# One order for VectorE's evacuations, weight sums and low parts, and an early last product in the second gate pair

## The chip, the cores and the metric

The kernel runs on one core of one Trainium2 chip. The metric is the time of one execution in microseconds (us) on the device; the kernel before takes 2360.54 us, the median of three executions. TensorE is PE in the profile, its weight loads PEld, VectorE is DVE, ScalarE is ACT, GpSimd is POOL, and SP is the engine that only issues transfers here.

## What is computed

The reference is a trunk of two layers over 512 frames of width 1024, all in fp32. What bears on the change is that nearly all of its work is matrix products of activations with weights:

```python
for i in range(DEPTH):
    h = rmsnorm(x, norm1_g[i])
    z = h @ w_in[i] + b_in[i]
    _, _, mv, mo, mi, mf, rq, rk, rv, rg, gm, gr = split_cols(z)
    ...
    hr = retention_chunkwise(rope(rq), rope(rk) / 16, rv, log_gamma)
    y_r = silu(rg) * head_layernorm(hr, r_norm_g[i], 4)
    merged = sigmoid(gm) * (y_m @ w_bm[i]) + sigmoid(gr) * (y_r @ w_br[i])
    x = x + merged @ w_out[i]
    h2 = rmsnorm(x, norm2_g[i])
    x = x + square(relu(h2 @ w_ff1[i] + b_ff1[i])) @ w_ff2[i] + b_ff2[i]
    h3 = rmsnorm(x, norm3_g[i])
    x = x + sigmoid(h3 @ w_pe_gate[i]) * (p[i] @ w_pe[i])
return rmsnorm(x, final_g)
```

Retention has four heads with values of width 512. Head h multiplies its normalised output by `silu(rg)`, 512 columns of `z`. These are the gates that the change speaks of.

## The kernel before

**Numbers in two parts.** Each fp32 operand is split into a high part in the rounded type that TensorE takes (ACT copies it, L277) and a low part, the rest (DVE subtracts, L278). A product is three matmuls: high by high, high by low, low by high. So each piece of weights, once loaded by SP into a raw tile (`wr`, four of them and at times a fifth), needs an ACT copy to `wh` and after it a DVE subtraction to `wl`. This is `prep_next` (L365), and `ready(k)` prepares pieces in one fixed list up to number k. The copies keep the order of the list among themselves, and so do the subtractions (`in_order`, L280). A raw tile is free for the next load when its last reader is through, and there are three tiles each for the high and the low parts of whole pieces, so a pair's B waits until the pair before is done with its own B.

**Units and pairs.** The weights are a list of units. T8 units (128 output columns) and V units are plain: one piece, products over all 512 frames. PAIR units cover 256 output columns and 1024 inputs as a 2 by 2 block scheme with seven half-size products in place of eight. A pair's weights are the pieces A, B, C and D (`PRODUCTS` and `PIECE`, from L91): A holds B11 and t1, B holds B21 and t2, C holds B22 and t3, D holds t4. The sums t1 and t3 are made by GpSimd transfers between DRAM tensors. For the feed-forward weights so are t2 and t4; for all other pairs (44 of the program) DVE makes t2 into B's raw tile out of the raw tiles of A and C (L379) and t4 out of B's raw tile (L381), before the ACT copy of that piece. So a pair's piece B has the chain: sum L379, copy L277, subtraction L278.

**The seven products and their banks.** `run_pair` (L433) issues P1, P5, P6, P2, P3, P7 and, later, P4. Each is twelve matmuls of 256 columns. Three PSUM banks are used: P1, P6, P7 and P4 accumulate one on top of the other in bank a, P5 and P3 in bank c, P2 is alone in bank b. After each product its bank is read out (an evacuation): in `pair_tiles` P1, P5, P6 and P4 by ACT (L476, L478, L482, L488), P2, P3 and P7 by DVE (L480, L484, L486, adding to what was read out before). The next product of a bank can't start before the evacuation of the one before is done. So P6 waits for P1's, P7 for P6's, P4 for P7's, P3 for P5's. Pieces are asked for by `READY`: ahead of P6 the next unit's first piece, ahead of P7 one piece more, which is B where the next unit is a pair.

P4 is not issued at once. It is put on the list `later`, and `flush` issues it at the next good place: in a next pair after its P1 and P5, in a T8 unit in the middle, in V units after the first, in the attention after the first rows. P4's evacuation hands the result to `consume`.

**The gates.** `r_out` (L988) makes a head's gates by two pairs, named o0 and o1 (w = 0, 1), each giving two tiles of 128 columns; `consume` puts Silu over them (ACT, L995). Then for v = 0 to 3 it transposes the head's output on TensorE (four transposes to a bank, `back`), multiplies it by gate tile v on DVE (L1006) and splits it. The last product of o1 comes with the `flush` after the transposes of v = 0. There are eight such places, four heads in two layers (l0r0o1 to l1r3o1 in the trace).

**Queries and keys.** `r_qk` makes a head's rotated queries and keys by two pairs one right behind the other, named brq and brk. `consume` is the rotation: six DVE instructions (L961 to L963) and two splits for each. Behind head 0's brk comes the gate pair bgm2.

**The feed-forward pairs.** `ff2` (L1265) is a pair whose evacuations all are DVE additions into `x` (L1272, L1274). It is named o with two numbers; l0o33 and l1o33 are the last of their layers, followed by the gate product `pg`.

**Who sets the order.** The framework in which the kernel is written lines up each engine's instructions when the program is built, by its own estimate of when each could start, and keeps the order of the code only where an edge says so. `tc.add_manual_dep(..., ORDER)` writes such an edge; it costs no wait, as both ends are on one engine. Before the change there are edges between copies, between subtractions and between weight loads. DVE's evacuations and sums have none: they can be put ahead of or behind any subtraction. [...]

Of the kernel before, what the change touches and what calls it, by code (L numbers as in the profile page):

```python
# [38 lines left out]
OP = mybir.AluOpType  # L39
SYNC = mybir.DependencyInfo(mybir.DependencyClass.Sync, mybir.DependencyReason.DATA)  # L40
ORDER = mybir.DependencyInfo(mybir.DependencyClass.NoSync, mybir.DependencyReason.DATA)
# [57 lines left out]
GIVEN = ("B11", "B12", "B21", "B22")  # L99
MADE = {"t1": ("B12", "B11"), "t3": ("B12", "B22"), "t2": ("t1", "B22"), "t4": ("t2", "B21")}  # L100

READY = {"P1": 2, "P4": 2, "P5": 3, "P2": 4, "P6": 4, "P3": 4, "P7": 5}


def due(k):
# [4 lines left out]
def in_dram(g):  # L110

    return g[1][0] == "f"
# [115 lines left out]
def build(ctx, tc, ins, out):  # L228
    nc = tc.nc
    ve, ac, gp, te = nc.vector, nc.scalar, nc.gpsimd, nc.tensor  # L230
# [17 lines left out]
    cur = {}  # L248
# [21 lines left out]
    def ps(name):  # L270
        return psum.tile([P, T], F32, name=name, tag="ps")
# [4 lines left out]
    def split(src, hi_ap, lo_ap):  # L276
        a = ac.activation(hi_ap, src, AF.Copy)  # L277
        return a, ve.tensor_sub(lo_ap, src, hi_ap.bitcast(F32))  # L278

    def in_order(kind, *new):  # L280

        for a, b in zip(cur.get(kind, ()), new):
            tc.add_manual_dep(b.ins, a.ins.name, ORDER, reason="order of the weights")
        cur[kind] = new


    index, given, sums, k = {}, {}, {}, 0
    for g, v in groups().items():
        index[g] = len(index)
# [46 lines left out]
    order = [(n, x) for n, u in enumerate(units) for x in (PIECE if u[0] == "PAIR" else (0,))]  # L336
    place = {x: k for k, x in enumerate(order)}
    loads = [(n, x) for n, u in enumerate(units) for x in (LOADS[in_dram(u[1])] if u[0] == "PAIR" else (0,))]
    raws, pieces = {}, {}
# [25 lines left out]
    def prep_next():  # L365
        n, x = order[at["prep"]]
        at["prep"] += 1
        fill_raws()

        w = Q if x == "D" else UN  # L370
        pl = cur["last"] if n >= NU - LAST else wpool
        kw = {"tag": "d", "bufs": 2} if x == "D" else {"tag": "l", "bufs": 2 * LAST} if pl is not wpool else {
            "tag": "w", "bufs": 2 * PIECES}
        out_ = [pl.tile([P, w], F32R, name=f"w{a}{n}_{x}", **kw) for a in "hl"]
        f, l = slice(0, Q), slice(Q, 2 * Q)
        if x in ("B", "C", "D") and not in_dram(units[n][1]):
            b = raws[n, "B"]
            if x == "B":
                ve.tensor_tensor(b[:, l], raws.pop((n, "A"))[:, l], raws[n, "C"][:, f], OP.add)  # L379
            elif x == "D":  # L380
                ve.tensor_tensor(b[:, f], b[:, f], b[:, l], OP.add)  # L381
            r = raws.pop((n, x)) if x == "C" else b
            if x == "D":
                del raws[n, "B"]
        elif x == "A" and not in_dram(units[n][1]):
            r = raws[n, x]
        else:
            r = raws.pop((n, x))
        in_order("prep", *split(r[:, :w], *out_))
        pieces[n, x] = out_  # L390

    def ready(k):
        while at["prep"] < min(len(order), k + 1):
            prep_next()
# [31 lines left out]
    later = []  # L426

    def flush():

        while later:  # L430
            later.pop()()

    def run_pair(name, act, done):  # L433

        n = next_unit()
        assert units[n][0] == "PAIR", units[n]
        bank = {}

        def product(x):
            w, half, j = PRODUCTS[x]  # L440
            ready(place[n, "A"] + READY[x])
            wh, wl = [a[:, half * Q:(half + 1) * Q] for a in pieces[n, w]]
            b = {"P2": "b", "P5": "c", "P3": "c"}.get(x, "a")
            first = x in ("P1", "P2", "P5")
            if first:
                bank[b] = ps(f"{name}{b}")
            o = bank[b][:, 0:S]
            for k in range(4):
                s = slice(k * P, (k + 1) * P)
                h, l = act[k](j)  # L450
                f, e = first and k == 0, k == 3
                te.matmul(o, wh[:, s], h, start=f, stop=False, skip_group_check=True)
                te.matmul(o, wh[:, s], l, start=False, stop=False, skip_group_check=True)
                cur["mm"] = te.matmul(o, wl[:, s], h, start=False, stop=e, skip_group_check=True)
            done(x, o)

        def last():
            product("P4")
            for w in PIECE:
                del pieces[n, w]  # L460

        product("P1")
        product("P5")
        flush()
        for x in ("P6", "P2", "P3", "P7"):
            product(x)
        later.append(last)

    def pair_tiles(name, act, consume, y=None):

        y = y or [tmp(f"{name}y{d}") for d in range(2)]
        a, b = slice(0, S), slice(S, T)

        def done(x, o):
            if x == "P1":
                ac.activation(y[0][:, b], o, AF.Copy)  # L476
            elif x == "P5":
                ac.activation(y[1][:, a], o, AF.Copy)  # L478
            elif x == "P2":
                ve.tensor_tensor(y[0][:, b], o, y[0][:, b], OP.add)  # L480
            elif x == "P6":
                ac.activation(y[1][:, b], o, AF.Copy)  # L482
            elif x == "P3":
                ve.tensor_tensor(y[1][:, b], o, y[1][:, b], OP.add)  # L484
            elif x == "P7":
                ve.tensor_tensor(y[1][:, a], o, y[1][:, a], OP.add)  # L486
            else:
                ac.activation(y[0][:, a], o, AF.Copy)  # L488
                consume(y)

        run_pair(name, act, done)

    def pair_operand(name, st, hi, lo):

# [120 lines left out]
    def bcol(i, n, k):  # L615
        o, _ = _B[n]
        return bc[:, i, o + k:o + k + 1]
# [185 lines left out]
    x = big("x0", F32)  # L803
# [17 lines left out]
    for i in range(L):  # L821
# [166 lines left out]
        def r_out(h, num, y):  # L988
            nm = f"l{i}r{h}o"
            gs = {}  # L990

            def gates(w):
                def consume(g):
                    for d in range(2):
                        ac.activation(g[d], g[d], AF.Silu, bias=bcol(i, "brg", 4 * h + 2 * w + d), scale=SIGN[d])  # L995
                        gs[2 * w + d] = g[d]

                return consume

            for w in range(2):  # L1000
                pair_tiles(f"{nm}{w}", xs, gates(w))
            for v in range(4):
                o = back(nm, num, v)
                if v == 0:
                    flush()
                ve.scalar_tensor_tensor(gs[v], o, bcol(i, "grn", 4 * h + v), gs[v], OP.mult, OP.mult)  # L1006
                split(gs[v], y[0][(4 * h) % 8 + v], y[1][(4 * h) % 8 + v])

# [41 lines left out]
        for d in range(4):  # L1050
            o = t8(xa, f"l{i}m0z{d}")
# [7 lines left out]
            a = (f"l{i}m0{d}", 8 * (d // 2) + d % 2, qk[2 * (d // 2)][d % 2], qk[2 * (d // 2) + 1][d % 2], d < 2, n1)  # L1059
# [24 lines left out]
        xs = sevenfold(xn, xs_t)  # L1084
# [55 lines left out]
        for c in range(KT):  # L1140
            o = t8(yr, f"l{i}br0{c}")
# [20 lines left out]
        for c in range(KT):  # L1162
# [6 lines left out]
            o = t8(yr, f"l{i}br1{c}")  # L1169
# [13 lines left out]
        if i == L - 1:  # L1183
            x_pool = phase("x", act_side)
            whole = x_pool.tile([P, KT, T], F32, name=f"l{i}x", tag="x")
            x = [whole[:, c, :] for c in range(KT)]
        else:
            x = big(f"l{i}x", F32)
# [17 lines left out]
        for c in range(KT):  # L1206
            o = t8((mh, ml), f"l{i}wo{c}")
# [54 lines left out]
        def tile3(c):  # L1262
            n3.tile(c, x[c])

        def ff2(b, p):  # L1265
            started = set()

            def add(q, o, op):
                y = x[2 * p + q // 2][:, (q % 2) * S:(q % 2 + 1) * S]
                if b == 0 and q not in started:  # L1270
                    started.add(q)
                    ve.scalar_tensor_tensor(y, y, bcol(i, "bf2", 2 * p + q // 2), o, OP.add, op)  # L1272
                else:
                    ve.tensor_tensor(y, y, o, op)  # L1274

            def done(x_, o):
                if x_ in ("P1", "P2"):
                    add(1, o, OP.add)
                elif x_ == "P5":
                    add(2, o, OP.subtract)  # L1280
                elif x_ in ("P6", "P3"):
                    add(3, o, OP.subtract)
                elif x_ == "P7":
                    add(2, o, OP.subtract)
                elif x_ == "P4":
                    add(0, o, OP.add)
                    if b == 3 and p == 3:
                        tile3(6)
                        tile3(7)
                if b == 3 and p and x_ in ("P6", "P7"):  # L1290
                    tile3(2 * p - 2 + (x_ == "P7"))

            def parts(k):
                h, l = hid[b, k]
                return lambda j: (h[:, j * S:(j + 1) * S], l[:, j * S:(j + 1) * S])

            run_pair(f"l{i}o{b}{p}", [parts(k) for k in range(4)], done)
# [20 lines left out]
        for u in range(2):  # L1318
            _, wh, wl = unit("PE")
            for c in range(4):  # L1320
                o = ps(f"l{i}pe{u}{c}")
# [11 lines left out]
        last = i == L - 1  # L1333
# [21 lines left out]
        for c in range(KT - LAST if last else KT):  # L1355
            o = t8(n3.act, f"l{i}pg{c}")
# [27 lines left out]
    for a, n in enumerate(nn):  # L1384
        for c in range(KT - LAST, KT):
            _, wh, wl = ws[c - KT + LAST]
            o = ps(f"pl{a}{c}")[:, :256]
# [134 lines left out]
```

## Time and profile before

| | |
|---|---|
| executions | 2364.43, 2360.54, 2360.48 us |
| span of the profiled execution | 2365.7 us (the page gives no other time of it) |
| TensorE busy | 2333.0 us, 99% |
| VectorE busy | 1697.9 us, 72% |
| ScalarE busy | 1256.4 us, 53% |
| granted TensorE clock, mean | 0.996 |

The profile is of one more execution, beside the three that were timed. Busy time is the union of an engine's instructions; a wait shows as idle time. "<-" names what ended an idle time. In names of tiles buffer numbers are left out, so `wr<-wr,wr` is a weight sum of whichever pair, and `wh_B`, `wl_B` are the high and low part of a piece B.

### The profile page before, as it was taken

To read this page: it belongs to the slowest core of one execution; us is meant where nothing else is said; L and a number is where in the kernel's file an instruction comes from. 1 tells how busy PE (TensorE), PEld (TensorE's weight loads), DVE (VectorE), ACT (ScalarE), POOL (GpSimd) and SP (SyncE) were. 2 spreads that over 40 slices of the span, in tenths; PEclk is the share of its full clock that TensorE was granted. 3 is DMA by queue.
4 is the path that set the end of the run, shared out by engine and by line. 5 is a ranking of instruction groups with operands and counts; after the bars stand their busy time and mean duration, and the time that the engine had idled before them with its cause. 6 is when DMAs were issued, how large, how long until landed. Compare 5 with 4: busy or idle time off the path is not lost.

```text
span 2365.7 us, 37058 instructions
## 1 busy us (share of the span) xinstructions
PE 2333.0 (99%) x14364; PEld 2095.7 (89%) x14364; DVE 1697.9 (72%) x2651; ACT 1256.4 (53%) x1864; POOL 251.1 (11%) x364
## 2 busy tenths in 40 slices
PE   9999999999999999999999999999999999999998
PEld 7888898888898899999888888999989988999997
DVE  6877577774666877777768785777738668777775
ACT  5756344553454656556457563445525547466554
POOL 4111100000000200000321110000000011000012
PEclk9999999999999999999999999999999999999999
DMA  6576775658578787866776657665574877654651
GB/s 217 169 192 176 218 210 168 163 163 237 159 219 279 222 224 230 230 201 204 216 198 167 183 158 216 183 159 163 156 217 140 244 229 206 208 155 147 187 153 53
DMA packets 173104, 450.52 MB, mean 190 GB/s; under 512 B 17136, under 2 KB 19568, under 8 KB 172928
## 3 DMA queue, kind: packets, MB, share of 16 engines
q1 hardware_dynamic: 117360, 269.76, 34.5%
q0 software_dynamic: 38144, 146.81, 27.0%
q10 hardware_dynamic: 17424, 31.59, 3.7%
q8 instruction: 112, 1.84, 0.3%
q14 instruction: 64, 0.52, 0.1%
HBM read 433.42 MB, written 161.48 MB: 251 GB/s over the span
## 4 chain that ended last, share of the span: by engine, by line
PE 90%; DMA 4%; DVE 3%; ACT 1%; issue 1%; SPq 0%; DVEq 0%; POOLq 0%; POOL 0%; ACTq 0%
DMA wr<-wpairs 2%; PE l0f L403 1%; PE l1f L403 1%; PE l0br L403 1%; PE l1f L404 1%; PE l1br L403 1%; PE l0br L405 1%; PE l1br L405 1%; PE l1br L404 1%; PE l0f L404 1%; PE l0br L404 1%; PE l1f L405 1%; PE l0f L405 1%; DMA wr<-s7t 1%; PE l1bm L403 1%
## 5 line engine op out<-in xcount | busy, mean ns | idle before, releaser
L277 ACT ACTIVATE wh<-wr 128x1024 fp32r<-128x1024 f32 x222 | 234.1, 1056 | 259.6 <-PE l1br L404 27.7
L278 DVE TENSOR_TENSOR wl<-wr,wh 128x1024 fp32r<-128x1024 f32 x222 | 272.6, 1229 | 118.0 <-ACT wh L277 112.9
L277 ACT ACTIVATE wh_C<-wr 128x1024 fp32r<-128x1024 f32 x92 | 97.4, 1059 | 159.8 <-PE l1bm L404 12.2
L277 ACT ACTIVATE wh_B<-wr 128x1024 fp32r<-128x1024 f32 x92 | 97.4, 1059 | 108.6 <-PE l1bm L405 4.7
L278 DVE TENSOR_TENSOR wl_B<-wr,wh_B 128x1024 fp32r<-128x1024 f32 x92 | 112.4, 1222 | 43.6 <-ACT wh_B L277 43.4
L278 DVE TENSOR_TENSOR wl_C<-wr,wh_C 128x1024 fp32r<-128x1024 f32 x92 | 112.2, 1220 | 32.2 <-ACT wh_C L277 32.2
L278 DVE TENSOR_TENSOR wl_A<-wr,wh_A 128x1024 fp32r<-128x1024 f32 x92 | 112.2, 1220 | 28.8 <-ACT wh_A L277 25.9
L277 ACT ACTIVATE wh_A<-wr 128x1024 fp32r<-128x1024 f32 x92 | 96.8, 1053 | 55.9 <-PE l0r1vp L656 4.4
L277 ACT ACTIVATE wh_D<-wr 128x512 fp32r<-128x512 f32 x92 | 57.7, 627 | 102.0 <-DVE wr L381 8.9
L278 DVE TENSOR_TENSOR wl_D<-wr,wh_D 128x512 fp32r<-128x512 f32 x92 | 63.3, 688 | 55.6 <-ACT wh_D L277 53.1
L379 DVE TENSOR_TENSOR wr<-wr,wr 128x512 f32<-128x512 f32 x44 | 30.2, 687 | 45.5 <-DMA wr<-wpairs 45.1
L403 PE MATMUL l0f<-l0n2h,wh 128*128 128x512 f32 x128 | 50.1, 391 | 0.0
L403 PE MATMUL l1f<-l1n2h,wh 128*128 128x512 f32 x128 | 50.0, 390 | 0.0
L405 PE MATMUL l1f<-l1n2h,wl 128*128 128x512 f32 x128 | 49.9, 390 | 0.0
L404 PE MATMUL l1f<-l1n2l,wh 128*128 128x512 f32 x128 | 49.9, 390 | 0.0
L405 PE MATMUL l0f<-l0n2h,wl 128*128 128x512 f32 x128 | 49.9, 390 | 0.0
L404 PE MATMUL l0f<-l0n2l,wh 128*128 128x512 f32 x128 | 49.8, 389 | 0.0
L573 POOL TENSOR_TENSOR l1n3sum<-l1n3sum,l1n3sq 128x512 f32<-128x512 f32 x6 | 8.2, 1371 | 263.3 <-ACT l1n3sum L565 240.8
L381 DVE TENSOR_TENSOR wr<-wr 128x512 f32<-128x512 f32 x44 | 30.0, 681 | 0.3
L405 PEld LDWEIGHTS l0f<-l0n2h,wl 128*128 128x128 f32 x128 | 24.0, 188 | 5.3 <-DVE wl L278 0.2
L405 PEld LDWEIGHTS l1f<-l1n2h,wl 128*128 128x128 f32 x128 | 24.0, 188 | 5.2 <-DVE wl L278 0.2
L403 PEld LDWEIGHTS l1f<-l1n2h,wh 128*128 128x128 f32 x128 | 24.0, 188 | 4.7
(6342 smaller groups left out, 9017.0 us busy)
## 6 DMA issues: line engine op xcount, KB each, us to landing
wr<-wstream SPq DMA_DIRECT2D x222, 512.0 KB, 4.7
wr<-wpairs SPq DMA_DIRECT2D x276, 256.0 KB, 3.6
s6t<-wpairs POOLq DMA_DIRECT2D x6, 1024.0 KB, 9.7
s7t<-wpairs POOLq DMA_DIRECT2D x6, 1024.0 KB, 9.4
s8t<-wpairs POOLq DMA_DIRECT2D x6, 1024.0 KB, 9.5
s9t<-wpairs POOLq DMA_DIRECT2D x6, 1024.0 KB, 8.9
s10t<-wpairs POOLq DMA_DIRECT2D x6, 1024.0 KB, 9.1
s11t<-wpairs POOLq DMA_DIRECT2D x6, 1024.0 KB, 9.6
```

The source lines that it names most:

```text
L277: a = ac.activation(hi_ap, src, AF.Copy)
L278: return a, ve.tensor_sub(lo_ap, src, hi_ap.bitcast(F32))
L379: ve.tensor_tensor(b[:, l], raws.pop((n, "A"))[:, l], raws[n, "C"][:, f], OP.add)
L381: ve.tensor_tensor(b[:, f], b[:, f], b[:, l], OP.add)
L403: te.matmul(o, sh, mh, start=first, stop=False)
L404: te.matmul(o, sh, ml, start=False, stop=False)
L405: cur["mm"] = te.matmul(o, sl, mh, start=False, stop=last)
L573: gp.tensor_tensor(self.sum, self.sum, sq, OP.add)
```

## The change

A new helper `turn` chains DVE instructions by order edges. In the chain go the evacuations of pairs by DVE, the additions of `ff2`, the sums L379 and L381, and every subtraction L278 of a weight piece, in the order of the code. All else on DVE (rotations, statistics, L1006, the norms) is left free. P7 asks for one piece less ahead of its matmuls, and for that piece after its evacuation (`AFTER`): so the next pair's L379 stands behind P7's evacuation in the chain. In the second gate pair (`at_once`) P7 goes ahead of P3, and P4 right behind P3; the products there are P1, P5, P6, P2, P7, P3, P4, then all transposes, with v in the order 0, 1, 3, 2.

```diff
-READY = {"P1": 2, "P4": 2, "P5": 3, "P2": 4, "P6": 4, "P3": 4, "P7": 5}
+READY = {"P1": 2, "P4": 2, "P5": 3, "P2": 4, "P6": 4, "P3": 4, "P7": 4}
+
+AFTER = {"P7": 5}
...
+    def turn(*new):
+
+        for b in new:
+            if "turn" in cur:
+                tc.add_manual_dep(b.ins, cur["turn"].ins.name, ORDER, reason="order of the pairs")
+            cur["turn"] = b
...
-                ve.tensor_tensor(b[:, l], raws.pop((n, "A"))[:, l], raws[n, "C"][:, f], OP.add)
+                turn(ve.tensor_tensor(b[:, l], raws.pop((n, "A"))[:, l], raws[n, "C"][:, f], OP.add))
...
-                ve.tensor_tensor(b[:, f], b[:, f], b[:, l], OP.add)
+                turn(ve.tensor_tensor(b[:, f], b[:, f], b[:, l], OP.add))
...
-        in_order("prep", *split(r[:, :w], *out_))
+        hi, lo = split(r[:, :w], *out_)
+        in_order("prep", hi, lo)
+        turn(lo)
...
             done(x, o)
+            if x in AFTER:
+                ready(place[n, "A"] + AFTER[x])
...
-        for x in ("P6", "P2", "P3", "P7"):
+        for x in ("P6", "P2", "P7", "P3") if at_once else ("P6", "P2", "P3", "P7"):
             product(x)
-        later.append(last)
+        if at_once:
+            last()
+        else:
+            later.append(last)
...
             for w in range(2):
-                pair_tiles(f"{nm}{w}", xs, gates(w))
-            for v in range(4):
+                pair_tiles(f"{nm}{w}", xs, gates(w), at_once=w == 1)
+            for v in (0, 1, 3, 2):
                 o = back(nm, num, v)
-                if v == 0:
-                    flush()
```

The evacuations of P2, P3 and P7 in `pair_tiles` (L480, L484, L486) and both additions of `ff2` (L1272, L1274) are wrapped in `turn(...)` in the same way.

More of the change, by code (lines that the diff above doesn't have):

```diff
@@ L431, in flush, with run_pair @@
             later.pop()()
-    def run_pair(name, act, done):
+    def run_pair(name, act, done, at_once=False):
         n = next_unit()
@@ L464, in run_pair, with pair_tiles @@
         flush()
-        for x in ("P6", "P2", "P3", "P7"):
+        for x in ("P6", "P2", "P7", "P3") if at_once else ("P6", "P2", "P3", "P7"):
             product(x)
-        later.append(last)
-    def pair_tiles(name, act, consume, y=None):
+        if at_once:
+            last()
+        else:
+            later.append(last)
+    def pair_tiles(name, act, consume, y=None, at_once=False):
         y = y or [tmp(f"{name}y{d}") for d in range(2)]
@@ L479, in done @@
             elif x == "P2":
-                ve.tensor_tensor(y[0][:, b], o, y[0][:, b], OP.add)
+                turn(ve.tensor_tensor(y[0][:, b], o, y[0][:, b], OP.add))
             elif x == "P6":
@@ L483, in done @@
             elif x == "P3":
-                ve.tensor_tensor(y[1][:, b], o, y[1][:, b], OP.add)
+                turn(ve.tensor_tensor(y[1][:, b], o, y[1][:, b], OP.add))
             elif x == "P7":
-                ve.tensor_tensor(y[1][:, a], o, y[1][:, a], OP.add)
+                turn(ve.tensor_tensor(y[1][:, a], o, y[1][:, a], OP.add))
             else:
@@ L489, in done @@
                 consume(y)
-        run_pair(name, act, done)
+        run_pair(name, act, done, at_once)
     def pair_operand(name, st, hi, lo):
@@ L1271, in add @@
                     started.add(q)
-                    ve.scalar_tensor_tensor(y, y, bcol(i, "bf2", 2 * p + q // 2), o, OP.add, op)
+                    turn(ve.scalar_tensor_tensor(y, y, bcol(i, "bf2", 2 * p + q // 2), o, OP.add, op))
                 else:
-                    ve.tensor_tensor(y, y, o, op)
+                    turn(ve.tensor_tensor(y, y, o, op))
             def done(x_, o):
```

## The prediction

> **What bounds the kernel now.** First the page's head and its busy line.
>
> ```profile
> span 2365.7 us, 37058 instructions
> ...
> PE 2333.0 (99%) x14364; PEld 2095.7 (89%) x14364; DVE 1697.9 (72%) x2651; ACT 1256.4 (53%) x1864; POOL 251.1 (11%) x364
> ```
>
> TensorE is idle for 2365.7 - 2333.0 = 32.7 us, and the change takes no matmul away. So it is worth what it takes from, or adds to, these 32.7 us and from time at a lowered clock. Next the waits of PE, longest first (waited in all, times, longest):
>
> ```profile
> PE l0r0o1a L452 <- DVE l0r0o1y L486: 4.4, 1, 4.4
> PE l1o33a L452 <- DVE l1x L1274: 1.7, 1, 1.7
> ...
> PE l0o33a L452 <- DVE l0x L1274: 1.5, 1, 1.5
> ...
> PE l0r0brqa L452 <- DVE l0r0brqy L486: 0.9, 1, 0.9
> PE l1r0brqa L452 <- DVE l1r0brqy L486: 0.8, 1, 0.8
> ```
>
> All of these are the same event: P4 waits in bank a until DVE has evacuated P7. What keeps DVE is seen in its timeline at the longest (start, duration, in brackets the idle time before and its releaser):
>
> ```profile
> 435.48 0.69 DVE L379 TENSOR_TENSOR wr<-wr,wr 128x512 f32<-128x512 f32 x1 [4.88 <-DMA wr<-wpairs]
> 436.09 0.42 DVE L484 TENSOR_TENSOR l0r0o1y<-l0r0o1c,l0r0o1y 128x256 f32<-128x256 f32 x1
> 436.42 1.21 DVE L278 TENSOR_TENSOR wl_B<-wr,wh_B 128x1024 fp32r<-128x1024 f32 x1
> 437.56 0.42 DVE L486 TENSOR_TENSOR l0r0o1y<-l0r0o1a,l0r0o1y 128x256 f32<-128x256 f32 x1
> ```
>
> DVE sat for 4.88 us on a weight sum of a pair still to come, whose load had not landed, and two evacuations (L484, L486) stood behind it. The free order had pulled the sum ahead of them. The change forbids just that.
>
> The eight gate places differ in how much they lose. These are windows from the last matmul of o1's P7 to the first matmul behind all transposes, one per head and layer; after the length come the busy times, then the granted clock:
>
> ```profile
> 432.64:442.70 10.06, 5.61 (x31) 5.37 (x30) 5.99 (x9) 3.95 (x6) 0.00 (x0) 0.66 0.50 176
> 513.70:518.64 4.94, 3.48 (x31) 3.25 (x30) 4.94 (x8) 3.13 (x5) 0.00 (x0) 1.00 0.04 15
> 633.14:638.04 4.90, 3.47 (x31) 3.23 (x30) 4.90 (x8) 3.12 (x5) 0.00 (x0) 1.00 0.05 20
> 663.40:666.83 3.43, 3.43 (x31) 3.23 (x30) 3.43 (x7) 3.01 (x5) 0.00 (x0) 1.00 0.70 272
> 1606.54:1610.69 4.15, 3.47 (x31) 3.23 (x30) 4.15 (x7) 3.12 (x5) 0.00 (x0) 1.00 0.07 27
> 1681.70:1686.42 4.72, 3.46 (x31) 3.22 (x30) 4.72 (x8) 3.12 (x5) 0.00 (x0) 1.00 0.05 17
> 1800.95:1804.77 3.82, 3.48 (x32) 3.24 (x30) 3.82 (x6) 3.13 (x5) 0.00 (x0) 1.00 0.05 17
> 1830.12:1833.57 3.45, 3.45 (x31) 3.25 (x30) 3.45 (x7) 3.01 (x5) 0.32 (x1) 1.00 0.29 109
> ```
>
> The work in them is the same; the shortest, 3.43 us, has TensorE busy throughout. Above it lie 6.63, 1.51, 1.47, 0, 0.72, 1.29, 0.39 and 0.02: 12.0 us in all. The first loses more than its 4.4 us of waiting because the clock falls to 0.66 of full over the window.
>
> **The change part by part.** Gain one, the gate places. With P7 ahead of P3, P4 has a whole product of cover where it had some transposes. Whether that is enough is read at l0r1o0 and o1, first TensorE, then DVE:
>
> ```profile
> 503.71 0.28 PE L454 MATMUL l0r1o0a<-l0xsh,wl_C 128*128 128x256 f32 x1
> ...
> 508.13 0.28 PE L452 MATMUL l0r1o1a<-l0xsh,wh_B 128*128 128x256 f32 x1
> ```
>
> ```profile
> 504.25 0.41 DVE L486 TENSOR_TENSOR l0r1o0y<-l0r1o0a,l0r1o0y 128x256 f32<-128x256 f32 x1
> ...
> 507.40 1.22 DVE L278 TENSOR_TENSOR wl_C<-wr,wh_C 128x1024 fp32r<-128x1024 f32 x1
> ...
> 511.24 0.42 DVE L480 TENSOR_TENSOR l0r1o1y<-l0r1o1b,l0r1o1y 128x256 f32<-128x256 f32 x1
> ```
>
> The last matmul of o0's P7 starts at 503.71; P1, P5 and o0's P4 follow, and o1's P6 starts at 508.13. So a product takes (508.13 - 503.71) / 3 = 1.47 us at most. An undisturbed evacuation starts 0.54 after the last matmul and takes 0.41: it is done after 0.95, and a product in between covers it with 0.5 to spare. I take all 12.0 us as gained there; less remains below.
>
> Gain two, P4 of head 0's brq: P3's and P7's evacuations now stand ahead of the sum of a later pair. 0.9 + 0.8 = 1.7 us. Gain three, the last feed-forward pairs:
>
> ```profile
> 1136.31 0.41 DVE L1274 TENSOR_TENSOR l0x<-l0x,l0o33c 128x256 f32<-128x256 f32 x1
> 1137.42 1.22 DVE L278 TENSOR_TENSOR wl<-wr,wh 128x1024 fp32r<-128x1024 f32 x1 [0.70 <-ACT wh L277]
> 1138.56 0.41 DVE L1274 TENSOR_TENSOR l0x<-l0x,l0o33a 128x256 f32<-128x256 f32 x1
> ```
>
> ```profile
> 2301.92 1.21 DVE L278 TENSOR_TENSOR wl<-wr,wh 128x1024 fp32r<-128x1024 f32 x1
> 2303.05 0.41 DVE L1274 TENSOR_TENSOR l1x<-l1x,l1o33a 128x256 f32<-128x256 f32 x1
> ```
>
> The subtraction between is the piece that P7 now asks for only after its evacuation. The evacuation moves up by 1138.56 - 1136.72 = 1.8 us in layer 0, where P4 waited 1.5, and by 2303.05 - 2301.92 = 1.1 in layer 1. That gives 1.5 + 1.1 = 2.6 us. The gains come to 12.0 + 1.7 + 2.6 = 16.3 us.
>
> The cost is that a pair's B is now made late. Its sum stands behind the previous pair's P7 evacuation, where the free order had made it a pair's length ahead, and P6 needs B three products later. The durations are in the page's groups (busy, mean ns of one):
>
> ```profile
> L277 ACT ACTIVATE wh_B<-wr 128x1024 fp32r<-128x1024 f32 x92 | 97.4, 1059 | 108.6 <-PE l1bm L405 4.7
> L278 DVE TENSOR_TENSOR wl_B<-wr,wh_B 128x1024 fp32r<-128x1024 f32 x92 | 112.4, 1222 | 43.6 <-ACT wh_B L277 43.4
> ...
> L379 DVE TENSOR_TENSOR wr<-wr,wr 128x512 f32<-128x512 f32 x44 | 30.2, 687 | 45.5 <-DMA wr<-wpairs 45.1
> ```
>
> At r1o1 this gives 504.25 + 0.41 + 0.69 + 1.06 + 1.22 = 507.63. P6 starts at 508.13 and needs the low part for its third matmul only, two of 1.47 / 12 = 0.12 later: slack 0.74. What is queued behind it, wl_C, could start at 507.63 in place of 507.40, a shift of 0.2; then P2's evacuation ends near 511.9, while P7's, in the place that P3 has now, falls due after 512.8. So fourteen such pairs (o1 and brk) cost nothing by this sum, if ACT takes the copy at once.
>
> ACT doesn't at head 0's o1, whose Silu needs another table:
>
> ```profile
> 423.93 1.28 ACT L995 ACT_TABLE_LOAD   x1
> ```
>
> The table load can go ahead of the copy of B. It then makes B 1.28 later against a slack of 0.74: 0.5, and with the Silu behind it some 0.6, in each layer. Between 0 (the copy goes first) and twice that I take 1.2 us for both. [...]
>
> The other place is the gate pair bgm2 behind head 0's brk, where DVE is full with rotations and there is no slack:
>
> ```profile
> 1490.25 1.21 DVE L278 TENSOR_TENSOR wl_B<-wr,wh_B 128x1024 fp32r<-128x1024 f32 x1
> ...
> 1491.14 0.28 PE L452 MATMUL l1bgm2a<-l1xsh,wh_B 128*128 128x256 f32 x1
> ...
> 1491.38 0.41 DVE L486 TENSOR_TENSOR l1r0brky<-l1r0brka,l1r0brky 128x256 f32<-128x256 f32 x1
> ```
>
> Now P7's evacuation comes at 1490.25, then the sum to 1491.35, the copy to 1492.41, the subtraction to 1493.63. P4 of brk can run from 1491.14 to 1492.61, and P6's third matmul then wants B at 1492.85: 0.8 short. With the 0.8 that TensorE arrives earlier (gain two) it is up to 1.6. I take 1.2 in each layer, 2.4 us. In the feed-forward pairs B comes ready-made from DRAM and only its subtraction moves behind P7's evacuation, 1.22 of the same slack; I put that at nothing, and between 2 us less and 2 more for its loads, which are issued as raw tiles come free.
>
> Sum: 16.3 - 1.2 - 2.4 = 12.7 us against the profiled execution: 2353.0. But its span is 5.2 above the median of the runs, and the 10.06 window is the one place that differs from its twin in layer 1 by about that: 6.63 - 0.72 = 5.9. Whether the load lands late there is chance. I take it that the timed runs mostly haven't got it. Then the gain is 12.7 - 5.9 = 6.8 us, and the forecast 2360.5 - 6.8 = 2353.7 us. If they have it, 2347.8.
>
> **The rivals.** Slower: *the fixed order holds up DVE in every pair*. DVE waits for ACT's copies at many subtractions, as the 43.4 in the row of wl_B shows, and in a chain no evacuation can use that time. It decides where the copy of B is late: from 0.74 on each of the sixteen o1 and brk pairs waits. What ACT could put ahead of it is in its timeline at o1:
>
> ```profile
> 504.87 0.71 ACT L995 ACTIVATE l0r1o0y<-l0r1o0y,bc 128x512 f32<-128x512 f32 x1
> 505.53 0.38 ACT L476 ACTIVATE l0r1o1y<-l0r1o1a 128x256 f32<-128x256 f32 x1
> ```
>
> If two of the 0.71 and one of the 0.38 go ahead of each copy, it is late by 1.8, and 16 x 1.06 = 17 us give 2370.7. ACT is busy for only 53% of the span, which speaks against; the full DVE at bgm2 speaks for. [...]
>
> No change, first way: *the wait moves*. The chain ahead of o1's P7 evacuation (four subtractions) runs late, and half of the gate gain without the chance event, 3 us, is lost: 2356.7. The 0.9 of margin computed speaks against. Second way: *the order built hardly differs*, as at the places that lose 0 and 0.02 now; what is gained at o33 and brq goes at bgm2: 2360.
>
> **How the numbers follow.** 0.2% is 4.7 us, about what a measurement of this kernel can tell from no change: below 2355.8 is faster, above 2365.3 slower. Forecast 0.62, of it 0.55 below 2355.8; the wait moves 0.15, of it 0.03 below; the order hardly differs 0.10; held up 0.13. Faster 0.58, same 0.29, slower 0.13. The range runs from 2346, below the case with the chance event, to 2365: left out are the slower rival and a tail of about 0.05.
>
> **What would show it.** Right: the waits of PE no longer list l0r0o1a to l1r3o1a, o33a and brqa; windows from the end of o1's P3 through the transposes are alike for all heads; L379's waits for DMA shrink from 45.1; new waits of PE for wl_B or wh_B at bgm2, about 1 us. Wrong: waits for B at many o1 and brk pairs, or L486 still ahead of P4 there.

## The result and the profile after

The changed kernel takes 2350.5 us (median of five executions, 2350.07 to 2352.01), the kernel before in the same session 2362.4 (2360.48 to 2367.41): a ratio of 0.9944, 95% interval 0.9932 to 0.9955. Measured once more, beside the second group of experiments, it took 2351.2 (2349.87 to 2354.49) against 2369.5, a ratio of 0.9919 (0.9905 to 0.9932). The forecast was 2353.7 with a range of 2346 to 2365: faster, as forecast, by more than the 6.8 us that it gave.

The head of the page after, and of the waits of PE the longest in the pairs with those at bgm2 (waited in all, times, longest):

```profile
span 2349.2 us, 37070 instructions
...
PE 2327.8 (99%) x14364; PEld 2092.4 (89%) x14364; DVE 1688.9 (72%) x2651; ACT 1250.2 (53%) x1864; POOL 252.8 (11%) x364
```

```profile
...
PE l0o02a L463 <- DVE l0x L1286: 1.5, 1, 1.5
...
PE l0bgm2a L463 <- ACT wh_B L279: 0.7, 1, 0.7
PE l1bgm2a L463 <- ACT wh_B L279: 0.7, 1, 0.7
...
PE l0bgm2c L463 <- ACT wh_C L279: 0.5, 1, 0.5
PE l1bgm2c L463 <- ACT wh_C L279: 0.5, 1, 0.5
```

TensorE's idle time fell from 32.7 to 21.4 us. No gate place, no brqa and no o33a is left in the list. The sum (now L388) no longer waits for a load, while the subtraction of B waits longer than its 43.6 before:

```profile
L280 DVE TENSOR_TENSOR wl_B<-wr,wh_B 128x1024 fp32r<-128x1024 f32 x92 | 113.2, 1231 | 57.5 <-ACT wh_B L279 57.1
...
L388 DVE TENSOR_TENSOR wr<-wr,wr 128x512 f32<-128x512 f32 x44 | 30.1, 683 | 0.0
```

Where the time went is read best from both traces cut into the same nine stretches of work, at the first matmul of the same tile: to bgm3 (with brq, brk and bgm2 of layer 0), the four heads with their gate places, the merge and the feed-forward, o33, the same for layer 1, and the end. Behind the length stand the busy times of PE, PEld, DVE, ACT and POOL, then the granted clock, the DMA share and GB/s. Before:

```profile
0.00:336.90 336.90, 332.76 (x1697) 283.22 (x1697) 244.63 (x426) 188.76 (x295) 64.04 (x123) 1.00 0.69 197
336.90:666.83 329.93, 322.60 (x2069) 294.81 (x2068) 222.09 (x340) 154.17 (x239) 21.77 (x30) 0.99 0.61 179
666.83:1121.83 455.00, 451.99 (x3050) 417.38 (x3048) 333.85 (x485) 256.26 (x353) 37.90 (x41) 1.00 0.78 227
1121.83:1145.12 23.29, 21.74 (x158) 19.85 (x156) 20.75 (x26) 12.28 (x19) 8.89 (x6) 1.00 0.79 227
1145.12:1510.86 365.74, 364.94 (x1835) 309.45 (x1835) 267.75 (x464) 199.13 (x309) 56.70 (x96) 1.00 0.67 187
1510.86:1833.57 322.71, 320.43 (x2069) 292.74 (x2068) 221.84 (x340) 153.78 (x239) 18.56 (x26) 1.00 0.58 168
1833.57:2296.31 462.74, 461.53 (x3133) 427.15 (x3132) 344.21 (x498) 261.72 (x360) 27.78 (x25) 1.00 0.64 191
2296.31:2309.58 13.27, 11.61 (x74) 9.82 (x72) 11.20 (x13) 6.86 (x12) 4.12 (x3) 1.00 0.57 193
2309.58:2365.70 56.12, 45.44 (x295) 41.29 (x294) 31.62 (x61) 23.45 (x46) 11.39 (x15) 0.90 0.15 47
```

After:

```profile
0.00:337.49 337.49, 332.21 (x1696) 282.70 (x1697) 244.57 (x425) 188.73 (x295) 64.34 (x123) 1.00 0.67 197
337.49:657.78 320.29, 320.29 (x2070) 292.80 (x2068) 219.70 (x337) 149.78 (x238) 21.49 (x30) 1.00 0.62 185
657.78:1112.77 454.99, 451.74 (x3050) 417.45 (x3048) 334.58 (x490) 256.95 (x354) 37.84 (x41) 1.00 0.76 227
1112.77:1133.97 21.20, 21.20 (x159) 19.66 (x157) 17.93 (x26) 12.59 (x19) 9.11 (x6) 1.00 0.82 248
1133.97:1500.22 366.25, 365.02 (x1836) 309.43 (x1835) 267.65 (x463) 199.28 (x309) 56.81 (x96) 1.00 0.64 186
1500.22:1820.50 320.28, 320.28 (x2069) 292.77 (x2068) 219.70 (x337) 149.67 (x238) 18.95 (x26) 1.00 0.57 170
1820.50:2282.35 461.85, 461.02 (x3133) 427.07 (x3132) 342.12 (x501) 262.57 (x361) 27.84 (x24) 1.00 0.62 191
2282.35:2293.61 11.26, 11.26 (x75) 9.83 (x73) 11.07 (x16) 7.09 (x12) 5.03 (x3) 1.00 0.66 215
2293.61:2349.20 55.59, 44.81 (x295) 40.67 (x294) 31.62 (x61) 23.56 (x46) 11.40 (x15) 0.91 0.15 51
```

In the second and the sixth stretch PE is now busy for their whole length, 320.29 and 320.28: no idle time of PE is left there. Against the prediction's terms, profile against profile (gain, in us):

| stretch | measured | predicted | out of |
|---|---|---|---|
| to bgm3, layer 0 | -0.6 | -0.3 | brq 0.9, bgm2 -1.2 |
| heads, layer 0 | 9.6 | 9.0 | gate places 9.6, table load -0.6 |
| feed-forward, layer 0 | 0.0 | 0 | |
| o33, layer 0 | 2.1 | 1.5 | |
| to bgm3, layer 1 | -0.5 | -0.4 | brq 0.8, bgm2 -1.2 |
| heads, layer 1 | 2.4 | 1.8 | gate places 2.4, table load -0.6 |
| feed-forward, layer 1 | 0.9 | 0 | |
| o33, layer 1 | 2.0 | 1.1 | |
| end | 0.5 | 0 | |
| sum | 16.5 | 12.7 | |

In most executions the time lies about 1.7 above the span: the second profile of the kernel before has a span of 2366.9 and a time of 2368.69, the second one of the changed kernel 2352.8 and 2354.49. So the execution before with the span of 2365.7 took about 2367.4, and 2367.4 - 16.5 = 2350.9 is what the profiled execution after took (2350.91).

### The profile page after: what moved, and what is told of

It is laid out like the page before. It is cut to its first block, busy times and chain, and to the rows that moved or that the text cites. A ratio compares the mean times of both kernels' runs of the same rounds, so it can differ in the third digit from the quotient of the medians.

```text
span 2349.2 us, 37070 instructions
## 1 busy us (share of the span) xinstructions
PE 2327.8 (99%) x14364; PEld 2092.4 (89%) x14364; DVE 1688.9 (72%) x2651; ACT 1250.2 (53%) x1864; POOL 252.8 (11%) x364
## 4 chain that ended last, share of the span: by engine, by line
PE 96%; DVE 1%; DMA 1%; ACT 1%; issue 0%; POOLq 0%; POOL 0%; DVEq 0%; SPq 0%; ACTq 0%
PE l0br L416 1%; PE l1br L416 1%; PE l1f L414 1%; PE l0f L414 1%; PE l0br L414 1%; PE l1br L414 1%; PE l0f L415 1%; PE l1f L415 1%; PE l1br L415 1%; PE l0br L415 1%; PE l1f L416 1%; PE l0f L416 1%; PE l0pg L414 1%; PE l0pg L415 1%; PE l1bm L414 1%; PE l0bm L415 1%
## 5 line engine op out<-in xcount | busy, mean ns | idle before, releaser
L280 DVE TENSOR_TENSOR wl_C<-wr,wh_C 128x1024 fp32r<-128x1024 f32 x92 | 112.2, 1220 | 12.7 <-ACT wh_C L279 12.4
L388 DVE TENSOR_TENSOR wr<-wr,wr 128x512 f32<-128x512 f32 x44 | 30.1, 683 | 0.0
L414 PEld LDWEIGHTS l0f<-l0n2h,wh 128*128 128x128 f32 x128 | 24.1, 188 | 4.8
```

What stands on the lines that cost most here:

```text
L388: turn(ve.tensor_tensor(b[:, l], raws.pop((n, "A"))[:, l], raws[n, "C"][:, f], OP.add))
L414: te.matmul(o, sh, mh, start=first, stop=False)
```

## The experiments

Three groups of kernels, each beside its own executions of the kernel before, which took 2367.4, 2369.5 and 2369.8 us there (medians of 23, 9 and 9). Each group ran on another chip, so times are compared within a group or by ratios.

**One place alone** (e1_one_place). In the kernel before, for l0r0o1 only, the next pair's sum behind P7's evacuation:

```diff
-            ready(place[n, "A"] + READY[x])
+            late = x == "P7" and name == "l0r0o1"
+            ready(place[n, "A"] + READY[x] - late)
...
             done(x, o)
+            if late:
+                cur["behind"] = cur["evac"]
+                ready(place[n, "A"] + READY[x])
...
+                if "behind" in cur:
+                    tc.add_manual_dep(t.ins, cur.pop("behind").ins.name, ORDER, reason="one sum")
```

> The kernel before with a single change: at the one gate place l0r0o1 the next pair's weight sum is asked for after P7's evacuation and tied behind it. All else is free as before. Theory 'the stall is in the timed runs too': the place loses 6.6 us over the shortest of the eight windows, so the time falls by about 6 (5 to 7) against the kernel before in the same runs. Rival, the prediction's assumption, that the profiled execution had this stall by chance and the timed ones mostly have not: 0.7 us, what the layer-1 twin loses, so no difference that can be told (0 to 1.5). In the profile either way: no wait of PE at l0r0o1a, no fall of the clock near 435 us, all other waits as before.

Measured 2360.7 against 2367.4, ratio 0.9976 (0.9967 to 0.9985): by the ratio 5.7 us less, between 3.5 and 7.8. PE no longer waits at l0r0o1a. The rival, that the timed executions mostly haven't got the stall, falls. DVE's timeline at the place in this kernel:

```profile
431.48 0.43 DVE L490 TENSOR_TENSOR l0r0o1y<-l0r0o1c,l0r0o1y 128x256 f32<-128x256 f32 x1 [1.02 <-PE l0r0o1c L457]
432.83 0.42 DVE L492 TENSOR_TENSOR l0r0o1y<-l0r0o1a,l0r0o1y 128x256 f32<-128x256 f32 x1 [0.92 <-PE l0r0o1a L457]
433.17 0.68 DVE L379 TENSOR_TENSOR wr<-wr,wr 128x512 f32<-128x512 f32 x1
...
435.19 0.69 DVE L379 TENSOR_TENSOR wr<-wr,wr 128x512 f32<-128x512 f32 x1 [0.68 <-DMA wr<-wpairs]
```

Two sums are seen. The next pair's runs at once behind the evacuation. The one that waits for its load is that of the pair after it, which the free order had pulled up by two pairs; its load lands at about the same moment as before (435.2, before 435.5), but by then no evacuation stands behind it.

**Is the stall the rule?** (g3_before_look: the kernel before, a second profile.)

> The kernel before, unaltered, for a second profile of it. Theory 'the late load at l0r0o1 is the rule': a wait of 3 us or more at l0r0o1a and a fall of the clock behind it, as in the first profile. Rival 'it was chance': below 1 us there.

Its time was 2368.7. The wait, then DVE, and then the granted clock (0.50, behind the busy times) in the window where the matmuls begin again:

```profile
PE l0r0o1a L452 <- DVE l0r0o1y L486: 4.3, 1, 4.3
```

```profile
435.25 0.69 DVE L379 TENSOR_TENSOR wr<-wr,wr 128x512 f32<-128x512 f32 x1 [4.71 <-DMA wr<-wpairs]
```

```profile
437.50:439.00 1.50, 1.21 (x5) 1.21 (x6) 1.50 (x3) 1.23 (x2) 0.00 (x0) 0.50 0.00 0
```

A wait of 4.3, where the first profile has 4.4, with the clock at 0.50 behind it. Together with e1 the stall belongs to the kernel before, in its timed executions too.

**The order alone** (e2_order_only). The changed kernel with o1 as before:

```diff
-        for x in ("P6", "P2", "P7", "P3") if at_once else ("P6", "P2", "P3", "P7"):
+        for x in ("P6", "P2", "P3", "P7"):
             product(x)
-        if at_once:
-            last()
-        else:
-            later.append(last)
+        later.append(last)
...
-            for v in (0, 1, 3, 2):
+            for v in range(4):
                 o = back(nm, num, v)
+                if v == 0:
+                    flush()
```

> The changed kernel without the early last product: the chain on VectorE and the piece asked for after P7 stay, but o1 keeps P3 before P7, and P4 comes behind the first transposes as before. Theory 'the order does it': P7's evacuation is done 0.95 us after its last matmul, and two groups of transposes cover about that, so nearly the whole gain is there: 10 to 12 us under the kernel before, within 2 us of the changed kernel. Rival 'the early product does it': only brq (1.7) and o33 (2.6) less what bgm2 costs (about 3) are gained, 1 to 2 us, and each of the eight gate places still waits 0.5 to 1.5.

2352.2 us, ratio 0.9935 (0.9921 to 0.9949): the whole gain, 15 us where 10 to 12 were expected. The window from P7's last matmul to the first one behind the transposes, which the prediction showed for the kernel before with 10.06 to 3.43 us, in head 0 of layer 0:

```profile
432.99:436.40 3.41, 3.35 (x30) 3.14 (x29) 2.66 (x5) 2.51 (x5) 0.00 (x0) 1.00 0.94 343
```

All eight heads have 3.40 to 3.46. The transposes were cover enough once nothing stood ahead of the evacuation.

**The early last product alone** (e3_once_only): the kernel before with the other half of the diff above, and no chain.

> The kernel before with only the early last product: o1 in the order P1, P5, P6, P2, P7, P3, P4 and the transposes in the order 0, 1, 3, 2; nothing is chained on VectorE. Theory 'the order does it': the sum that waits for its load and a subtraction still stand ahead of P7's evacuation at l0r0o1, so the wait of 4.4 there stays at 3.5 to 5, and the six places that lose 0.4 to 1.5 lose less: 2 to 5 us gained in all. Rival 'the early product does it': a whole product of cover is enough everywhere, all eight places are free, 10 to 12 us gained.

2366.5 us, ratio 1.000 (0.9991 to 1.001): nothing gained, less than either theory gave. Its profile is of its slowest execution (2374.2), so not all of the waits in it need be in the others. PE's longest waits, and DVE at l0r0o1:

```profile
PE l0r0o1a L452 <- DVE l0r0o1y L489: 4.6, 1, 4.6
PE l0o33a L452 <- DVE l0x L1275: 4.0, 1, 4.0
PE l0gr1a L452 <- DVE l0gr1y L489: 3.0, 1, 3.0
```

```profile
435.63 0.69 DVE L379 TENSOR_TENSOR wr<-wr,wr 128x512 f32<-128x512 f32 x1 [4.29 <-DMA wr<-wpairs]
436.24 1.22 DVE L278 TENSOR_TENSOR wl_B<-wr,wh_B 128x1024 fp32r<-128x1024 f32 x1
437.37 0.42 DVE L489 TENSOR_TENSOR l0r0o1y<-l0r0o1a,l0r0o1y 128x256 f32<-128x256 f32 x1
437.70 0.41 DVE L487 TENSOR_TENSOR l0r0o1y<-l0r0o1c,l0r0o1y 128x256 f32<-128x256 f32 x1
```

P4 has a product of cover, 1.4 us, and the sum ahead of the evacuation waits three times that. The heads take 329.03 and 322.62 us in this profile, 1.0 less in all than before.

**The sums alone** (g1_sums_only): the kernel before with `AFTER`, and each sum L379 tied behind P7's evacuation; no other edge.

```diff
-                ve.tensor_tensor(b[:, l], raws.pop((n, "A"))[:, l], raws[n, "C"][:, f], OP.add)
+                t = ve.tensor_tensor(b[:, l], raws.pop((n, "A"))[:, l], raws[n, "C"][:, f], OP.add)
+                if "evac" in cur:
+                    tc.add_manual_dep(t.ins, cur["evac"].ins.name, ORDER, reason="sums behind")
```

> The kernel before with one rule only: the next pair's sum is asked for after P7's evacuation and tied behind it, for all pairs; evacuations, subtractions and the last product stay free as before. Theory 'the sums in front of the evacuations were the loss, and the subtraction that follows a sum': the eight gate places and brq are free, o33, where a subtraction of ready-made pieces is in front, still waits its 1.5 and 1.7, and bgm2 pays its 1.2 per layer: 10 to 14 us below the kernel before in the same runs, 2 to 4 above the chain alone. Rival 'the subtractions must be tied as well': the six gate places that lose 0.4 to 1.5 keep that, and only l0r0o1 is won, 5 to 7 us below the kernel before.

2358.4 us, ratio 0.9954 (0.9941 to 0.9966): 11 us less than before. The heads of layer 0 (layer 1: 320.46 too), and the waits that stay:

```profile
337.03:657.49 320.46, 320.40 (x2070) 292.71 (x2068) 219.81 (x336) 149.24 (x238) 21.77 (x30) 1.00 0.63 184
```

```profile
PE l0o01a L456 <- DVE l0x L1280: 1.9, 1, 1.9
PE l0o33a L456 <- DVE l0x L1280: 1.8, 1, 1.8
...
PE l1o33a L456 <- DVE l1x L1280: 1.5, 1, 1.5
```

The sums, with the subtraction that has to follow each, were all that the gate places lost: with the whole chain (e2) the same stretches take 320.50 and 320.45. Tying evacuations and other subtractions as well is worth 4.8 us, profile against profile with e2, where 2 to 4 were expected: 3.8 in the two stretches of o33, 1.2 in the feed-forward of layer 1, and 0.2 back elsewhere. By the ratios it is 4.5, with intervals that overlap.

**The sum ahead of the evacuation, in a chain** (e4_sum_first, and g4_sum_first_look for a second profile): the changed kernel with `"P7": 5` and an empty `AFTER`.

> The changed kernel with the chain and the early product, but with P7 asking for the next pair's B ahead of its matmuls again: in the chain the sum and the subtraction stand before P7's evacuation. Theory 'what stands ahead of the evacuation decides, not that there is a chain': sum 0.69, copy 1.06 and subtraction 1.22 make the evacuation about 0.9 late at each of the eight gate places, and at l0r0o1 the late load holds it up by some 4 more, while bgm2 gets its piece in time again (3 less): 5 to 10 us above the changed kernel. Rival 'any fixed order does': within 2 us of it, or below by the 3 us of bgm2.

> The kernel with the sum ahead of P7's evacuation in the chain, unaltered, for a second profile: its first one showed no wait at the gate places at 2353.6 us, while the other executions took up to 2362.5. Theory 'its slower executions are those where a load lands late and P7's evacuation stands behind its sum': a slower execution shows a wait of P4 or P3 for an evacuation at a pair ahead of a summed one, of 2 us or more, and a lowered clock behind. Rival: the time above 2353 lies in waits of the feed-forward pairs (l0o01 to l0o32) alone.

2356.9 us (2353.64 to 2362.52), ratio 0.9958 (0.9944 to 0.9972), 4.7 above e2 in the same group; the second look took 2356.0. Neither profile lists a wait at a gate place. But the evacuation is late there, as these rows of l0r1o1 show (last matmul of P7, transposes, P7's evacuation, first matmul of P4):

```profile
506.64 0.28 PE L465 MATMUL l0r1o1a<-l0xsh,wl_C 128*128 128x256 f32 x1
508.05 1.91 PE L728 MATMUL l0r1ot<-ident,l0r1num 128*128 128x128 f32 x16
509.42 0.42 DVE L502 TENSOR_TENSOR l0r1o1y<-l0r1o1a,l0r1o1y 128x256 f32<-128x256 f32 x1
509.89 0.39 PE L463 MATMUL l0r1o1a<-l0xnh,wh_D 128*128 128x256 f32 x1
```

The evacuation starts 2.8 us after the last matmul. At the eight places in both profiles it is 2.0 to 2.8, in the changed kernel 0.3 to 1.1: it is held up by more than the 0.9 that was expected, and P4 starts right behind it. TensorE has no idle time by that: its order is built anew too and now has transposes between P3 and P4. So what stands ahead of the evacuation does decide when it runs; whether TensorE waits depends on what else was put there. The late load of the sum two pairs ahead isn't seen at l0r0o1: in the chain that sum stands behind the evacuation. The waits at bgm2 stayed (0.9 and 0.5), though they were expected to go. The heads take 321.44 and 321.41 us in the first profile, 1.1 more each than in the changed kernel, all of it busy time of PE, which is not explained.

An execution as slow as its slowest, 2362.5, is in neither profile; what those lose stays open.

**The slack of B** (f4_double_copy): the changed kernel with the copy of a summed B done twice.

```diff
+        if x == "B" and not in_dram(units[n][1]):
+            ac.activation(out_[0], r[:, :w], AF.Copy)
         hi, lo = split(r[:, :w], *out_)
```

> The changed kernel with the copy of B done twice on ScalarE for the 44 pairs whose B is summed on VectorE, so that B comes 1.06 us later; the values are the same. It prices the slack. Theory of the prediction, slack 0.74 at o1 and brk: 0.32 late at fourteen pairs (4.5 us), 1.06 at head 0's o1 and at bgm2 in both layers (4.2 us): 7 to 9 us above the changed kernel. Rival 'no slack', the one that was to hold VectorE up: 1.06 at all of eighteen places, 17 to 19 us above. Third way, 'other matmuls fill in', since TensorE's order is built too and takes the parts of P6, P2 and P3 that need no low part: 0 to 3 us above.

2361.8 against 2351.2 for the changed kernel in the same group: 10.5 more, where the theory had 7 to 9. brq to bgm2 and the heads of layer 0:

```profile
294.78:340.57 45.79, 42.46 (x301) 39.17 (x300) 33.28 (x47) 23.35 (x36) 2.38 (x3) 1.00 0.71 195
340.57:662.13 321.56, 321.17 (x2069) 293.17 (x2068) 217.60 (x336) 162.35 (x251) 22.35 (x30) 1.00 0.64 183
```

The heads lose 321.56 - 320.29 = 1.3 us for the seven pairs that follow right on another, 0.2 each. No slack would have cost 7.4, so that rival is refuted there. The theory's slack of 0.74 gives 0.32 at six of them and 1.06 at head 0's o1, 3.0 in all: the slack is larger than that, or other matmuls fill in, as the third way has it. No run separates the two. Around bgm2 the second copy costs 3.2 (42.60 without, below): PE waits 1.4 at bgm2, 0.8 at the bm unit behind it and 0.7 at brk, of which only the first had been counted.

**Repairing bgm2.** First B asked for ahead of P3 in head 0's brk (f2_early_b), and the same with C a product later in all pairs (f3_early_b_late_c):

```diff
-            ready(place[n, "A"] + READY[x])
+            ready(place[n, "A"] + READY[x] + (early and x == "P3"))
...
+                pair_tiles(f"{nm}{bn}", xs, rope(a, bn), early=a == 1 and h == 0)
...
-READY = {"P1": 2, "P4": 2, "P5": 3, "P2": 4, "P6": 4, "P3": 4, "P7": 4}
+READY = {"P1": 1, "P4": 2, "P5": 3, "P2": 4, "P6": 4, "P3": 4, "P7": 4}
```

(the last two lines in f3 alone). The changed kernel was run again beside them (f1_after_again).

> The changed kernel once more, unaltered, as the yardstick of the three kernels beside it. Expected 11 to 15 us under the kernel before in the same runs (it was 11.9 under by the medians of its first runs; the kernel with the chain alone was 15.3 under).

> The changed kernel, but head 0's brk asks for bgm2's B one product earlier, ahead of P3's matmuls, so that in the chain the sum and the subtraction stand before P3's evacuation, not behind P7's. Theory 'bgm2 waits because its sum stands behind P3's and P7's evacuations': the waits of 0.7 (for the copy of B) and 0.5 (for that of C) in each layer go, 2.4 to 3 us less than the changed kernel. Rival 'VectorE is full there whatever the order': the wait only moves, to P5 or P4 of these pairs or to the rotations, and the time stays within 1 us of the changed kernel.

> As the run before, and in all pairs piece C is asked for one product later (by P5 in place of P1), so that its subtraction stands behind the evacuation of P1 in the chain. Theory 'at l0o02 and l0o32 P6 waits because P1's evacuation stands behind the subtraction of a C that is loaded late': these waits of 1.5 and 0.9 go, 4 to 5 us less than the changed kernel with the 2.4 of bgm2. Rival 'C is then late itself': P7 or P3 waits for wl_C in the gate pairs and the feed-forward pairs, 0.3 us or more at many of the 92 pairs, so slower than the changed kernel by several us.

The changed kernel 2351.2, f2 2351.8 and f3 2351.2: no difference, the rival's outcome for f2 and that of neither theory nor rival for f3, whose l0o02a still waited 1.8 while l0o32a's 0.9 was gone. The changed kernel was 18 us under the kernel before, more than the 11 to 15 expected. In f2 the waits at bgm2 stayed (0.8 and 0.5): the sum had come forward by 1.4 us only, still behind the whole rotation of brq and P2's evacuation, and in TensorE's order, which is built as well, P6 had moved ahead of brk's P4 in return. So the sum alone was put earlier, ahead of P2's evacuation, and the subtraction left in its place (g2_sum_ahead; `sum_b` issues the sum, in the chain):

```diff
             ready(place[n, "A"] + READY[x])
+            if early and x == "P6":
+                sum_b(n + 1)
```

> The changed kernel, but bgm2's sum alone stands early in the chain, ahead of the evacuation of P2 of head 0's brk; its subtraction stays behind P7's evacuation. Theory 'the sum's late place among the rotations is what bgm2 waits for': the copy of B begins some 2 us earlier, the waits of 0.7 and 0.5 in each layer go, 2 to 3 us below the changed kernel (2351.2). Rival 'VectorE is full there': the subtraction of B is late in its place and PE waits for wl_B or for P4's bank for as long; within 1 us of the changed kernel.

2348.2 us (2347.29 to 2350.30), ratio 0.9913 (0.9899 to 0.9927). From brq to the end of bgm2 in layer 0, first the changed kernel, then this one:

```profile
294.89:337.49 42.60, 41.38 (x301) 39.04 (x300) 33.38 (x47) 20.61 (x33) 2.38 (x3) 1.00 0.72 208
```

```profile
294.71:336.20 41.49, 41.49 (x301) 39.13 (x300) 33.22 (x47) 20.34 (x33) 2.37 (x3) 1.00 0.78 214
```

PE is busy for the whole 41.49; the waits at bgm2 are gone from the list, 1.1 us in each layer. The best times of this study are its own, 2 to 3 us below the changed kernel's medians, but the intervals of the two ratios overlap: shown in the profile, likely in the time.

## Why the prediction came out as it did

**The mechanism** was right, and is shown from both sides: sums ahead of the evacuations were what P4 waited for (g1, e1), and leaving the order out takes the gain away (e3). By its signs: the waits at o1, o33 and brq left the list; the windows from the end of o1's P3 through the transposes are 3.11 to 3.23 us for all heads; L388 waits no more; the new waits at bgm2 came with 0.7 and 0.5 where about 1 was named. VectorE kept to its order at l0r0o1: in e3 two evacuations stood behind one sum that waited 4.29 us for its load. The prediction left open whose sum this was; e1 shows it to be that of the pair after the next.

**Gain one, the gate places**, 12.0 us: measured 9.6 + 2.4, to the tenth. But the part-by-part account credited it to P7's place ahead of P3, "P4 has a whole product of cover". That step was wrong: e2 has the gain without it and e3 next to nothing with it. Beside the chain the early last product does nothing that was measured; whether it helps where the evacuation is late, as in e4, no run shows.

**The timed runs.** The step that failed for the size is "I take it that the timed runs mostly haven't got it". e1 and the second profile show the stall of l0r0o1 in the executions of the kernel before. With it in, the sum gave 2347.8, and the measured 2350.5 lies between that and 2353.7. Part of the error is that a span was set beside a median of times: the profiled execution was 6.9, not 5.2, above the median of 2360.5. That 2353.7 came within 3.2 us is partly luck: the gain was put at 6.8 where the medians of that session give 11.9 and the profiles 16.5, but the median that it was taken from is the lowest that the kernel before had. That the two shortest of the three times shown, 2360.5, had no stall would fit e1's 5.7 us, but no profile of such an execution was seen; why this kernel's medians went from 2360.5 to 2369.8 between sessions and chips, while the changed one kept to 2350.5 and 2351.2, stays open.

**The table load** of head 0's o1, 1.2 us: measured 0. PE is busy throughout the heads' stretches. ACT after, and then the row that follows the load in the kernel before:

```profile
421.17 1.28 ACT L1011 ACT_TABLE_LOAD   x1
424.03 0.73 ACT L1011 ACTIVATE l0r0o0y<-l0r0o0y,bc 128x512 f32<-128x512 f32 x1 [1.58 <-DVE l0r0o0y L502]
424.68 1.06 ACT L279 ACTIVATE wh_B<-wr 128x1024 fp32r<-128x1024 f32 x1
```

```profile
425.22 0.72 ACT L995 ACTIVATE l0r0o0y<-l0r0o0y,bc 128x512 f32<-128x512 f32 x1
```

The load has long been done when the copy of B becomes due; the Silu alone goes ahead of it. In the kernel before the load ran from 423.93 to 425.21, and the Silu started at 425.22, 0.01 us behind it. After, the load took the same 1.28 us, and the next activation waited 1.58 for DVE.

**bgm2**, 1.2 in each layer: PE waits 0.7 + 0.5 there, so the size was right, and g2 shows the cause, the place of the sum among the rotations. **o33**, 2.6: measured 4.1. All of the idle time in the two stretches went, 23.29 - 21.74 = 1.55 and 13.27 - 11.61 = 1.66, where the prediction, counting one subtraction, took 1.1 of the second; another 0.5 and 0.35 are busy time, which is not explained. **The feed-forward** was put at 0 with 2 on either side and came out at 0.0 and 0.9. The 0.0 of layer 0 is not the rule: in the second profile of the changed kernel that stretch took 458.35 us, 3.4 more than before (the last section has why). **The slower rival**, a chain that holds VectorE up in every pair, is refuted by the times and by the slack that f4 found; its claim that there is none holds at bgm2 alone, of the places looked at.

## What to carry to other kernels

When an engine waits with other work queued behind it, look at what waits and for whom: an instruction for a far stage that depends on a load doesn't belong ahead of an evacuation, and one order edge per such instruction brought most of the gain here (g1: a ratio of 0.9954, the whole chain 0.9935). Before giving a consumer more cover, see whether the producer is late by a little or stuck behind something else: cover of 1.4 us did next to nothing against a sum that waited 4.3 for its load (e3), while in e4 a product and transposes hid an evacuation that started 2.0 to 2.8 us after its own product. And where a list of waits is empty, look at the rows too: with an edge on one engine the planner can line up the others anew (as in f2 and e4), and so hide a late instruction behind other work. Set a profile's span against the time of the same execution before deciding that an event in it was chance.

## What the hardware showed beside this

The granted clock fell after waits of 1.9 to 2.4 us, with PE busy for the whole of the 2.00 us windows shown behind them. In the order alone (e2) PE waited 2.1 us at l0o02a, in the changed kernel 1.5, and these are windows right behind, first of e2, then of the changed kernel:

```profile
866.00:868.00 2.00, 2.00 (x11) 2.00 (x12) 2.00 (x4) 0.03 (x1) 0.00 (x0) 0.55 0.92 281
```

```profile
866.00:868.00 2.00, 2.00 (x19) 2.00 (x19) 2.00 (x4) 0.00 (x0) 0.00 (x0) 1.00 0.98 299
```

The clock is 0.55 there in place of 1.00, with 11 matmuls in 2 us in place of 19. The same fall, to 0.50 and 0.56, came behind a wait of 1.9 in g1 and of 2.4 in the changed kernel's second profile, none behind 1.8 in f3, where it stayed at 1.00. l0o02a is also where the changed kernel's two profiles differ: the feed-forward stretch of layer 0 took 454.99 us in the first and 3.4 more in the second, with 0.9 more of waiting at l0o02a and the lowered clock behind it.
